# A two-layer hybrid decoder step on one core: adaLN slabs moved between stages, output projection in half contractions, attention scaling moved to another engine

## The chip, the core and the metric

The kernel runs on one core of one Trainium2 chip. The metric is the device time of one execution in microseconds (us); a measurement is the median over several executions. Engines: PE is TensorE (matrix products), DVE is VectorE, ACT is ScalarE, POOL is GpSimd, SP is SyncE, whose queue issues nearly all the weight loads. Each engine works through its own instructions in order.

## The reference

Two layers with the same structure, for 512 prompt tokens and 8 sample sequences of 4 tokens, model width 1024:

```python
mod = silu(c) @ w_ada + b_ada                     # adaLN: 1024 x 6144 per layer
sh1, sc1, g1, sh2, sc2, g2 = split(mod, 6)
h = rms_norm(x, norm1) * (1 + sc1) + sh1
q, k, v, u, xr, yg = split(h @ w_in)              # 1024 x 1536
o_attn = window_attention(q, k, v, sinks)         # 8 heads, window 128
o_ssm, o_lru = s5(u), rg_lru(xr, yg)
o = concat(rms_norm(o_attn), rms_norm(o_ssm), rms_norm(o_lru)) @ w_o
x = x + g1 * o
h2 = rms_norm(x, norm2) * (1 + sc2) + sh2
gate, val = split(causal_conv3(h2 @ w_up))        # 1024 x 5632
x = x + g2 * ((gelu(gate) * val) @ w_down)        # 2816 x 1024
```

## The kernel before

Activations lie with 128 features on the partitions, eight chunks of features, and 544 tokens (512 prompt, 32 sample) on the free axis, in two halves of 256 and 288 tokens. A float32 product is made from three products of rounded parts: weight `whi` with data `hh` and `hl`, weight `wlo` with data `hh` (`mm3`, line 430). One unit is 128 output features: 8 chunks x 3 products x 2 halves = 48 matmuls.

Weights come in the class `Weights`: SP loads 512 KB into one of three `raw` buffers (line 412), ACT casts it to `whi` (415), DVE subtracts to `wlo` (416), into one of six slots. When a unit is done its slot goes to the next weight in a fixed order.

The stages of a layer are: a preamble (layer 0 only: x, the first adaLN slabs, the norm); the mixer (12 units of the input projection with chains of attention, SSM and LRU work drawn in between, then the rest of these chains, here called the tail); the output projection (`proj`, 8 units x 2 halves; `KO` gives the order of its eight chunks of contraction: 6, 7, 4, 5 are SSM and LRU outputs, 0 to 3 attention outputs); and the ffn (44 units of the up-projection in three parts, and after each part a share of the down-projection).

The adaLN product is made of slabs: 512 KB of `w_ada` each, loaded into the same `raw` buffers, then four matmuls of 32 x 256 (line 524; a row of the trace counts one slab as x8). Eight slabs fill one result of 8 chunks, which ACT copies out (531), PE transposes (536) and DVE adds to the bias (543). There are 48 slabs per layer. Layer 0's first 16 are in the preamble, four of them loaded as pieces of 512 bytes (line 502). The remaining 32 of layer 0 and the first 16 of layer 1 are drawn between the work of mixer 0, the last 32 of layer 1 between the work of mixer 1 (`background`). The ffn has none.

In the attention, a unit is two heads by 128 queries. Its scores (matmul, line 1242) go through a masked maximum on DVE (1244), an exponential on ACT, a reciprocal on DVE (1251) and a scaling on DVE, which is two calls of `ts` (line 384), then to the transposes on PE (1263). One small copy for the sinks on DVE stands ahead of it (1241).

PSUM results that PE writes are named by bank: `mb0s`, `mb1s` (mixers), `fb0w`, `fb0s`, `fb1w` (ffn) and `wide`. The number in a name is the layer.

Of the kernel before, what the change touches and what calls it, by code (L numbers as in the profile page):

```python
# [19 lines left out]
L = 2  # L20
# [4 lines left out]
KC = 8  # L25
# [16 lines left out]
KO = (6, 7, 4, 5, 0, 1, 2, 3)  # L42
NATT = 1
AHEAD = 7
SPARE = (4, 5, 9, 11)
PIN = True
S12 = (2, 14, 5, 16)
SQN = (0, 10)
NHN = [9, 17]
S3 = 1  # L50
# [13 lines left out]

PRM = {}
_n = 0
for _name, _w in (
# [10 lines left out]
    "wada": (L, 3, 8, 2, 128, 4, 256), "win": (L, 12, 128, 8, 128), "wo": (L, 8, 128, 8, 128),  # L78
# [56 lines left out]
def layout(I):  # L135
# [43 lines left out]
    A["wada"] = I["w_ada"].reshape(L, 8, 128, 3, 4, 2, 256).transpose(0, 3, 1, 5, 2, 4, 6)  # L179
# [137 lines left out]
def trunk(ctx: ExitStack, tc: tile.TileContext, A, O):  # L317
# [173 lines left out]
    def ada_slabs(l, banks, ahead, spare=()):  # L491
        d = LY[l]
        todo = [(bank, k, hf) for bank in banks for hf in range(2) for k in range(8)]
        have = {}

        def fetch(n):
            if n < len(todo) and n not in have:
                bank, k, hf = todo[n]
                if n in spare:
                    have[n] = [T(512) for _ in range(2)]  # L500
                    for a, t in enumerate(have[n]):
                        nc.sync.dma_start(t.rearrange("p (g c) -> p g c", g=4),
                                          A["wada"][l, bank, k, hf, :, :, 128 * a:128 * a + 128])
                    return
                raw = wp.tile([128, 8, 128], F32, tag="raw", name="raw", bufs=NRAW)
                have[n] = raw.rearrange("p (g a) c -> p g (a c)", g=4)
                nc.sync.dma_start(have[n], A["wada"][l, bank, k, hf])

        for n, (bank, k, hf) in enumerate(todo):
            for m in range(n, n + ahead + 1):  # L510
                fetch(m)
            if k == 0:
                if bank == 0 and hf == 0:
                    d["mod"] = lp.tile([128, 48, 9], F32, name="mod")
                ps = one(256)
            if n in spare:
                for a, t in enumerate(have[n]):
                    for g in range(4):
                        T_.matmul(ps[32 * g:32 * g + 32, 128 * a:128 * a + 128], silu[:, k, :],
                                  t[:, 128 * g:128 * g + 128], start=False, stop=k == 7, skip_group_check=True)  # L520
                free(*have[n])
            else:
                for g in range(4):
                    T_.matmul(ps[32 * g:32 * g + 32], silu[:, k, :], have[n][:, g],  # L524
                              start=k == 0, stop=k == 7, skip_group_check=True)
            del have[n]
            yield 1
            if k < 7:
                continue
            row = W(256)  # L530
            S.copy(row, ps)
            PS.put(ps)
            yield 1
            pt = one(256)
            for c in range(2):
                T_.transpose(pt[:, c * 128:c * 128 + 128], row[:, c * 128:c * 128 + 128], eye)

            def part(t):
                return t[:, bank * 16:bank * 16 + 16].rearrange("p (g h c) r -> p g h c r", g=4, h=2)[:, :, hf]

            src = pt.rearrange("p (c g r) -> p g c r", c=2, g=4)[:, :, :, 0:9]
            b = d["prm"]("bada")[:, :, None].to_broadcast([128, 48, 9])
            V.tensor_tensor(part(d["mod"]), src, part(b), op=OP.add)
            PS.put(pt)
            d["ada"] = (bank, hf)
            for al, at, bk in (("al1", 8, 0), ("al2", 32, 2)):
                if bk == bank:
                    alpha(l, al, "norm" + al[2], at, hf)
            yield 1
# [300 lines left out]
    def norm_half(hf, al, sh):  # L850
# [3 lines left out]
        for c in KORD:  # L854
            t = W(w)
            V.tensor_mul(t, x[:, c, a:b], nr)
# [6 lines left out]
            V.tensor_sub(hs[c][1][:, a:b], t, f32(hs[c][0][:, a:b]))  # L863
            yield

    def norm_all(hf, al, sh):
        yield from norm_stats(hf)
        for _ in norm_half(hf, al, sh):
            pass
# [362 lines left out]
    def att_S(l, M, u):  # L1232
# [8 lines left out]
        V.tensor_copy(pm[:, :, nk:nk + 1], d["nsink"][:, c, :, None])  # L1241
# [10 lines left out]
        for g in range(2):  # L1252
            ts(pm[:, g, 0:nk], pm[:, g, 0:nk], st[:, 2, g:g + 1])
# [173 lines left out]
    bg = []  # L1427

    def background(n=1):
        for _ in range(n):  # L1430
            while bg:
                try:
                    next(bg[0])
                    break
                except StopIteration:
                    bg.pop(0)

    def flush():
        while bg:
            background()  # L1440

    def mixers(l, pool):
        d = LY[l]
        mod = d["mod"]
        sh1 = mod[:, 0:8]
        M = Mix()
        M.pool = pool
        M.win_done = M.back = False
        M.units, M.pipe, M.left = ([], []), [None, None], [8, 9]
        M.r, M.o, M.g, M.hl = {}, set(), [None, None], [None, None]  # L1450
# [4 lines left out]
        M.sq, M.part = {}, {}  # L1455
        M.kz = const("kz", (128, 2, NP), pool=pool)
        M.ks = const("ks", (128, NS), pool=pool)
        for g in range(2):
            G.memset(M.kz[64 - 64 * g:128 - 64 * g, g], 0.0)
# [352 lines left out]
```

## Time and profile before

| | |
|---|---|
| runs | 1328.3, 1330.35, 1334.8 us; median 1330.35 us |
| the profiled execution | 1335.0 us, span 1333.2 us |
| PE / DVE / ACT busy | 95% / 66% / 43% of the span |
| mean granted TensorE clock | 0.992 |
| preamble | 0 to about 65 us |
| mixer 0 and output projection | to about 296 us; tail from 191 to 244 us |
| ffn of layer 0 | about 296 to 698 us |
| mixer 1 and output projection | to about 930 us; tail from 843 to 878 us |
| ffn of layer 1 | to the end |

The profiled execution is the slowest of those shown, 0.35% above the median. Busy shares are means over stages; a stage is read from its own rows.

### The profile page before, as it was taken

The page shows a single profiled execution, that of the slowest core. Times are in us where ns is not written, and L with a number is a line of the kernel's source. Part 1 is how long each engine was busy: PE and PEld are TensorE (multiplying, and loading weights), DVE is VectorE, ACT ScalarE, POOL GpSimd, SP SyncE. Part 2 cuts the span into 40 slices and gives each one's busy share as a digit, 9 for nine tenths or more (in the row PEclk, how much of TensorE's full clock was granted, in tenths as well). Part 3 has the DMA queues.
Part 4 walks back from the last instruction along what each step waited for, and adds up shares of the span by engine and source line. Part 5 has one row for each costly group of instructions (what it writes and reads, how often), then busy time and mean ns, then how long its engine had stood idle before and what let it go on. Part 6 is the DMA issues. An engine that isn't in the chain of part 4 may idle for free.

```text
span 1333.2 us, 26368 instructions
## 1 busy us (share of the span) xinstructions
PE 1270.1 (95%) x10438; PEld 1164.8 (87%) x10438; DVE 881.8 (66%) x2583; ACT 576.5 (43%) x1112; POOL 48.8 (4%) x82
## 2 busy tenths in 40 slices
PE   4899988999999999999999999899999999999998
PEld 2666765799999999999998776679999999999998
DVE  8787885988774556456576877668865456545651
ACT  4557544356542343234354466545643234313430
POOL 0021010000020000000000001000000000000000
PEclk9899999999999999999999999999999999999999
DMA  8876677533343223334235846602322332233221
GB/s 294 279 265 215 191 252 229 178 111 118 93 135 125 85 86 87 97 93 115 76 108 180 268 142 203 191 14 90 110 81 86 96 95 74 86 97 94 85 72 51
DMA packets 72460, 178.24 MB, mean 134 GB/s; under 512 B 15584, under 2 KB 26752, under 8 KB 72336
## 3 DMA queue, kind: packets, MB, share of 16 engines
q1 hardware_dynamic: 65456, 162.08, 39.1%
q0 software_dynamic: 4960, 11.68, 2.5%
q10 hardware_dynamic: 1920, 2.79, 0.7%
q8 instruction: 82, 1.34, 0.4%
q14 instruction: 42, 0.34, 0.1%
HBM read 159.37 MB, written 14.34 MB: 130 GB/s over the span
## 4 chain that ended last, share of the span: by engine, by line
PE 83%; DMA 9%; DVE 5%; ACT 2%; issue 1%; POOL 0%; SPq 0%; DVEq 0%; POOLq 0%; ACTq 0%
PE wide L430 42%; PE fb1w L430 9%; PE fb0w L430 8%; DMA raw<-in_wada_dram 6%; PE fb0s L430 5%; PE fb1s L430 4%; PE mb0s L430 3%; PE mb1s L430 3%; PE mb0s L524 1%; PE mb1s L524 1%; DMA raw<-in_wo_dram 1%; DVE wlo L416 1%; DMA f<-in_ssmh_dram 1%; DMA tab_br<-f 1%; PE mb1s L1242 0%
## 5 line engine op out<-in xcount | busy, mean ns | idle before, releaser
L430 PE MATMUL wide<-hh,whi 128*128 128x288 f32 (+1 forms) x1360 | 400.3, 295 | 1.2 <-ACT hh L897 0.8
L430 PE MATMUL wide<-hl,whi 128*128 128x288 f32 (+1 forms) x1360 | 395.9, 291 | 0.0
L430 PE MATMUL wide<-hh,wlo 128*128 128x288 f32 (+1 forms) x1360 | 394.3, 290 | 0.0
L416 DVE TENSOR_TENSOR wlo<-raw,whi 128x1024 fp32r<-128x1024 f32 (+1 forms) x176 | 211.0, 1200 | 187.1 <-ACT whi L415 183.1
L415 ACT CAST whi<-raw 128x1024 fp32r<-128x1024 f32 (+1 forms) x176 | 180.4, 1029 | 274.8 <-PE wide L430 125.8
L430 PEld LDWEIGHTS wide<-hh,whi 128*128 128x128 f32 x1360 | 257.2, 189 | 18.3 <-issue 14.0
L430 PEld LDWEIGHTS wide<-hl,whi 128*128 128x128 f32 x1360 | 257.1, 189 | 6.3 <-issue 6.1
L430 PEld LDWEIGHTS wide<-hh,wlo 128*128 128x128 f32 x1360 | 259.2, 191 | 3.0 <-issue 3.0
L380 DVE SCALAR_TENSOR_TENSOR f<-wide,prm,f 128x511 f32<-128x511 f32 x236 | 100.2, 485 | 0.0
L430 PE MATMUL wide<-mid,whi 128*128 128x256 f32 (+1 forms) x526 | 99.8, 287 | 0.0
L430 PEld LDWEIGHTS wide<-mid,whi 128*128 128x128 f32 x526 | 82.4, 188 | 0.0
L897 ACT CAST mid<-f 128x544 fp32r<-128x544 f32 x44 | 28.5, 647 | 122.4 <-DVE f L1660 119.1
L430 PE MATMUL wide<-mid,wlo 128*128 128x256 f32 (+1 forms) x263 | 75.5, 287 | 0.0
L377 ACT ACTIVATE f<-f 128x544 f32<-128x544 f32 x50 | 33.0, 659 | 89.2 <-DVE f L1650 84.5
L430 PE MATMUL fb1w<-hh,whi 128*128 128x256 f32 (+1 forms) x240 | 69.4, 289 | 1.8 <-ACT hh L862 1.3
L430 PE MATMUL fb1w<-hl,whi 128*128 128x256 f32 (+1 forms) x240 | 69.4, 289 | 0.0
L430 PE MATMUL fb1w<-hh,wlo 128*128 128x256 f32 (+1 forms) x240 | 68.8, 287 | 0.0
L430 PE MATMUL fb0w<-hh,whi 128*128 128x256 f32 (+1 forms) x224 | 64.7, 289 | 1.6 <-ACT hh L862 1.1
L430 PE MATMUL fb0w<-hl,whi 128*128 128x256 f32 (+1 forms) x224 | 64.7, 289 | 0.0
L430 PE MATMUL fb0w<-hh,wlo 128*128 128x256 f32 (+1 forms) x224 | 64.3, 287 | 0.0
L430 PE MATMUL fb0s<-mid,whi 128*128 128x288 f32 (+1 forms) x326 | 62.9, 290 | 0.0
L430 PE MATMUL fb1s<-mid,whi 128*128 128x288 f32 (+1 forms) x308 | 59.1, 289 | 0.0
(612 smaller groups left out, 2542.2 us busy)
## 6 DMA issues: line engine op xcount, KB each, us to landing
raw<-in_wada_dram SPq DMA_DIRECT2D x92, 512.0 KB, 5.2
raw<-in_wup_dram SPq DMA_DIRECT2D x88, 512.0 KB, 3.5
raw<-in_wdn_dram SPq DMA_DIRECT2D x32, 448.0 KB, 3.3
raw<-in_win_dram SPq DMA_DIRECT2D x24, 512.0 KB, 4.2
raw<-in_wo_dram SPq DMA_DIRECT2D x16, 512.0 KB, 4.5
raw<-in_wdn_dram SPq DMA_DIRECT2D x16, 512.0 KB, 3.5
e<-q ACTq DMA_DIRECT2D x32, 68.0 KB, 4.6
out_ox_dram<-x SPq DMA_DIRECT2D x8, 272.0 KB, 2.1
```

What stands on the lines that cost most here:

```text
L377: return S.activation(out, in_, f, bias=bias, scale=scale, **kw)
L380: return V.scalar_tensor_tensor(out, a, s, b, op0=op0, op1=op1, **kw)
L415: S.copy(hi, raw)
L416: V.tensor_sub(lo, raw, f32(hi))
L430: T_.matmul(out, w[wi][:, k, :], r[ri][:, a:b], start=first and i == 0, stop=last and i == 2)
L524: T_.matmul(ps[32 * g:32 * g + 32], silu[:, k, :], have[n][:, g], start=k == 0, stop=k == 7, skip_group_check=True)
L897: S.copy(dst[0], src)
```

## The change

- **Slabs.** The layout of `w_ada` in memory becomes six parts of eight slabs per layer. Layer 0's parts 0 and 1 stay in the preamble, parts 2, 3 and 4 in mixer 0. Part 5 of layer 0 and all six parts of layer 1, 56 slabs, go to the up-projection of layer 0's ffn as 28 pairs: one load of 1 MB into one buffer `araw`, its eight matmuls at once, one step for each unit that ends. Mixer 1 has none.
- **First loads.** The 16 slabs of the preamble are loaded at once, into tiles that are free then (`q`, `kz`, `xc`, `gate`, `glu`, `e`, `f`), without pieces of 512 bytes; the second half of x follows the first eight. The rotation tables of the SSM (`ssm_rot(0)`) are issued on their engine after the first norm chunks, and the norm of the first half has a shorter form in `norm_all`.
- **Output projection.** Units 0 to 3 are accumulated in two parts: chunks 6, 7, 4, 5 first, which are added to x, and later chunks 0 to 3, added again. Their weights come as two loads of 256 KB. Units 4 to 7 are as before.
- **Attention.** The sinks' copy goes from DVE to ACT, and the scaling becomes an ACT activation (`Copy` with a per-partition scale).

```diff
+WO = ((4, 8, range(4)), (0, 4, range(4)), (0, 8, range(4, 8)))
...
+    def ada_pairs(l, parts, raw, bank):
...
+        def fetch(part, k):
+            nc.sync.dma_start(raw, A["wada"][l, part, k:k + 2].rearrange("k p g c -> p k g c"))
+
+        fetch(*todo[0])
+        yield 1
+        for n, (part, k) in enumerate(todo):
...
+            for i in range(2):
                 for g in range(4):
...
+                    T_.matmul(ps[32 * g:32 * g + 32], silu[:, k + i, :], raw[:, i, g],
+                              start=k + i == 0, stop=k + i == 7, skip_group_check=True)
+            if n + 1 < len(todo):
+                fetch(*todo[n + 1])
             yield 1
...
+            if k == 6:
+                yield from ada_end(l, part, ps)
...
-        V.tensor_copy(pm[:, :, nk:nk + 1], d["nsink"][:, c, :, None])
+        S.copy(pm[:, :, nk:nk + 1], d["nsink"][:, c, :, None])
...
-            ts(pm[:, g, 0:nk], pm[:, g, 0:nk], st[:, 2, g:g + 1])
+            act(pm[:, g, 0:nk], pm[:, g, 0:nk], AF.Copy, scale=st[:, 2, g:g + 1])
...
+            with tc.issue_after(LY[0]["first"]):
+                for _ in ssm_rot(0):
+                    pass
...
+        def some(i, hf, ks, last=True):
+            for k in ks:
+                need(k, hf)
+            o = one(HALF[hf][1] - HALF[hf][0], True, PLAST[0] if (i, hf) in PLAST[1] else ())
+            for k in ks:
+                part(o, i, hf, k, k == ks[0], k == ks[-1])
+            end(i, hf, o, last)
+            tick()
...
+        for i in range(4):
+            for hf in range(2):
+                if (i, hf) not in ((0, 0), (1, 0), (2, 0)):
+                    some(i, hf, KO[:4], False)
...
+                have = {k: ada_load(0, 0, k, homes[k]) for k in range(8)}
+                W_.ahead(GRP)
+                fetch_x(1)
...
-            bg.append(ada_slabs(l, (1, 2), 1))
+            if l == 0:
+                bg.append(ada_slabs(0, (2, 3, 4), 1))
...
+                if l == 0:
+                    bga.append(ada_pairs(0, (5,), raw, "fb0s"))
+                bga.append(ada_pairs(l + 1, range(6), raw, f"fb{l}s"))
```

SP's queue in the preamble, before and then of the change. In the names `x` is the input, `raw` and `f` hold slabs, and `in_win` is the input projection's weight.

```order
L1752 DMA x<-in_x_dram 128x4x256 x2
L1755 DMA eye<-in_eye_dram 128x128
L1756 DMA gm<-in_gm_dram 128x12
L507 DMA raw<-in_wada_dram 128x1024 x4
L502 DMA f_89<-in_wada_dram 128x4x128
L502 DMA f_90<-in_wada_dram 128x4x128
L502 DMA f_91<-in_wada_dram 128x4x128
L502 DMA f_92<-in_wada_dram 128x4x128
L507 DMA raw<-in_wada_dram 128x1024 x2
L412 DMA raw<-in_win_dram 128x1024 x3
L1752 DMA x<-in_x_dram 128x4x288 x2
```

```order
L1811 DMA x<-in_x_dram 128x4x256 x2
L1814 DMA eye<-in_eye_dram 128x128
L1815 DMA gm<-in_gm_dram 128x12
L530 DMA raw<-in_wada_dram 128x1024 x3
L526 DMA q<-in_wada_dram 128x512 x4
L526 DMA kz<-in_wada_dram 128x512 x2
L526 DMA xc_146<-in_wada_dram 128x512
L526 DMA xc_147<-in_wada_dram 128x512
L526 DMA gate<-in_wada_dram 128x512
L526 DMA glu<-in_wada_dram 128x512
L413 DMA raw<-in_win_dram 128x1024 x3
L1811 DMA x<-in_x_dram 128x4x288 x2
```

Ahead of the input projection's weights there were eight slabs, two of them in pieces, through four buffers; now there are eight through tiles of their own, and the other eight follow x.

SP's queue in layer 0's up-projection, of the change, with what each load waits for (a suffix of the semaphores' names is left as printed). `in_wup` is the up-projection's weight.

```order
L413 DMA raw<-in_wup_dram 128x1024 [waits DMAHW5_49,DVE_49,Activation_49]
L566 DMA araw<-in_wada_dram 128x2x1024 [waits PE_49]
L413 DMA raw<-in_wup_dram 128x1024 [waits DMAHW6_49,DVE_49]
L566 DMA araw<-in_wada_dram 128x2x1024 [waits DMAHW1_49,PE_49]
L413 DMA raw<-in_wup_dram 128x1024 [waits DMAHW7_49,DVE_49]
```

The loads of pairs wait for PE's matmuls on the pair before, and stand between loads of weights, which wait for DVE. Before the change this part of the queue has only the weights.

PE in the tail of mixer 1, before and then of the change. `kz`, `q` are an attention unit's scores, `eye,pm` the transposes of its probabilities, the rows of L430 and L431 the output projection.

```order
L430 MATMUL mb1s_7977<-hh_82,wlo_110 128x256
L524 MATMUL mb1s_7974<-raw,cin 32x256 x11
L1277 MATMUL wide_70<-g_7979,vt 64x128 x4
L1263 MATMUL mb1s_7975<-eye,pm 128x128 x2
L1242 MATMUL wide_71<-kz,q 128x512
L1359 MATMUL mb1s_7974<-f_93,f_90 32x128 x4
```

```order
L431 MATMUL mb1s_8112<-hh_82,wlo_114 128x288
L1317 MATMUL wide_70<-g_8114,vt 64x128 x4
L1303 MATMUL wide_71<-eye,pm 128x128 x2
L1282 MATMUL mb1s_8111<-kz,q 128x512
L431 MATMUL mb1s_8112<-hh_84,whi_115 128x288
L431 MATMUL mb1s_8112<-hl_85,whi_115 128x288
L431 MATMUL mb1s_8112<-hh_84,wlo_116 128x288
L431 MATMUL mb1s_8112<-hh_86,whi_115 128x288
```

Where slabs stood between the attention units, half contractions of the output projection stand now: five of 12 matmuls in each layer's tail, beside the three that were there.

## Rows read from the trace of the kernel before

**Rows 1.** The page, busy time and share of the span by engine

```profile
PE 1270.1 (95%) x10438; PEld 1164.8 (87%) x10438; DVE 881.8 (66%) x2583; ACT 576.5 (43%) x1112; POOL 48.8 (4%) x82
```

**Rows 2.** The page, chain that ended last, by engine

```profile
PE 83%; DMA 9%; DVE 5%; ACT 2%; issue 1%; POOL 0%; SPq 0%; DVEq 0%; POOLq 0%; ACTq 0%
```

**Rows 3.** Busy us (instructions) of each engine by stretch, clock, DMA

```profile
0.00:44.00 44.00, 21.89 (x180) 10.39 (x180) 35.65 (x209) 16.34 (x36) 3.58 (x10) 0.96 0.91 309
135.00:191.00 56.00, 52.99 (x490) 41.56 (x484) 47.49 (x181) 31.32 (x62) 3.64 (x4) 1.00 0.69 207
191.00:244.00 53.00, 43.98 (x425) 26.04 (x423) 33.77 (x150) 23.83 (x68) 2.10 (x2) 0.94 0.76 247
315.00:698.00 383.00, 382.68 (x3109) 381.85 (x3110) 231.65 (x501) 147.52 (x246) 12.52 (x23) 1.00 0.34 102
720.00:790.00 70.00, 64.47 (x624) 52.47 (x626) 51.87 (x140) 31.36 (x51) 4.75 (x8) 0.98 0.78 238
790.00:843.00 53.00, 51.56 (x416) 39.23 (x408) 38.44 (x143) 35.55 (x82) 4.71 (x4) 1.00 0.52 159
843.00:878.00 35.00, 28.54 (x238) 17.79 (x236) 25.12 (x107) 18.17 (x58) 0.00 (x0) 1.00 0.49 155
```

**Rows 4.** The same for line 430 alone, in the two tails

```profile
191.00:244.00 53.00, 4.94 (x25) 4.03 (x23) 0.94 0.76 247
843.00:878.00 35.00, 4.85 (x36) 4.46 (x36) 1.00 0.49 155
```

**Rows 5.** The same for line 524 alone (slab matmuls)

```profile
48.00:191.00 143.00, 19.85 (x200) 5.05 (x200) 0.99 0.73 229
191.00:244.00 53.00, 14.64 (x160) 4.26 (x160) 0.94 0.76 247
700.00:843.00 143.00, 18.63 (x192) 4.58 (x192) 0.99 0.63 195
843.00:878.00 35.00, 5.71 (x64) 1.82 (x64) 1.00 0.49 155
```

**Rows 6.** TensorE's waits, 48 to 300 us, then 700 to 935

```profile
PE mb0s L524 <- DMA raw<-in_wada_dram: 7.3, 6, 2.4
PE mb0s L1263 <- DVE pm L384: 3.8, 3, 1.5
PE wide L524 <- DMA raw<-in_wada_dram: 1.3, 1, 1.3
...
PE mb1s L524 <- DMA raw<-in_wada_dram: 9.3, 10, 1.7
```

**Rows 7.** Timeline: one slab, and two in a row

```profile
72.07 0.64 PE L524 MATMUL mb0s<-raw,cin 128*32 128x256 f32 x8
...
219.44 1.07 PE L524 MATMUL wide<-raw,cin 128*32 128x256 f32 x16
```

**Rows 8.** Chain of waits in the up-projection, start, us, what

```profile
451.00 6.01 PE fb0w L430 x48
```

**Rows 9.** Lines, 48:300, then two of 135:300 by shape

```profile
L377 ACT ACTIVATE half<-half,mod,al 128x256 f32<-128x256 f32 x16 | 8.9, 595 | 1.3 <-DVE half L856 1.1 <-DVE al L380 0.2
L384 DVE TENSOR_SCALAR pm<-pm,st 128x256 f32<-128x256 f32 (+1 forms) x32 | 9.4, 332 | 0.1
...
L1265 ACT COPY f<-wide 128x256 f32<-128x256 f32 x1 | 0.4, 372 | 0.1
L380 DVE SCALAR_TENSOR_TENSOR x<-mb0s,mod,x 128x256 f32<-128x256 f32 x12 | 5.7, 482 | 3.9 <-PE mb0s L430 3.7
```

**Rows 10.** The page, DMA issues: count, KB each, us to landing

```profile
raw<-in_wada_dram SPq DMA_DIRECT2D x92, 512.0 KB, 5.2
raw<-in_wup_dram SPq DMA_DIRECT2D x88, 512.0 KB, 3.5
raw<-in_wdn_dram SPq DMA_DIRECT2D x32, 448.0 KB, 3.3
```

**Rows 11.** TensorE's waits, 0 to 66 us

```profile
PE wide L524 <- DMA raw<-in_wada_dram: 10.7, 4, 8.9
```

More of the change, by code (lines that the diff above doesn't have):

```diff
@@ L496, in fetch, with ada_slabs @@
+    def ada_slabs(l, parts, ahead, have=None):
+        d = LY[l]
+        todo = [(part, k) for part in parts for k in range(8)]
+        have = have or {}
         def fetch(n):
             if n < len(todo) and n not in have:
[L498 to L509, printed above, removed]
+                have[n] = ada_load(l, *todo[n])
+        for n, (part, k) in enumerate(todo):
             for m in range(n, n + ahead + 1):
@@ L512, in ada_slabs @@
             if k == 0:
-                if bank == 0 and hf == 0:
+                if part == 0:
                     d["mod"] = lp.tile([128, 48, 9], F32, name="mod")
                 ps = one(256)
[L516 to L522, printed above, removed]
+            for g in range(4):
+                T_.matmul(ps[32 * g:32 * g + 32], silu[:, k, :], have[n][g // 2][:, g % 2],
+                          start=k == 0, stop=k == 7, skip_group_check=True)
@@ L530, in ada_slabs @@
[L530 to L549, printed above, removed]
+            if k == 6:
+                yield from ada_end(l, part, ps)
     def alpha(l, al, n, at, hf):
@@ L1466, in mixers @@
             setattr(M, n, const(n, sh, pool=pool))
+        return M
+    def mixers(l, M):
+        d = LY[l]
+        mod = d["mod"]
+        sh1 = mod[:, 0:8]
+        M.win_done = M.back = False
+        M.units, M.pipe, M.left = ([], []), [None, None], [8, 9]
+        M.r, M.o, M.g, M.hl = {}, set(), [None, None], [None, None]
+        M.sq, M.part = {}, {}
+        for g in range(2):
+            G.memset(M.kz[64 - 64 * g:128 - 64 * g, g], 0.0)
+        AR.names.update((t.tensor.name, t) for t in M.xt)
         CH = M.CH = Chains()
@@ L1549, in need, with part, end @@
             raise RuntimeError(("never ready", k, hf, M.left))
-        def end(i, hf, o):
+        def part(o, i, hf, k, first, last):
+            a = 0 if i > 3 or k < 4 else 4
+            mm3(o, W_[("wo", l, a, i)], k - a, hs[k], HALF[hf], first, last)
+        def end(i, hf, o, last=True):
             with urgent():
@@ L1566, in proj @@
         for i, hf in skewed(GRP):
[L1567 to L1574 removed]
+            some(i, hf, KO if i > 3 else KO[4:])
             if (i, hf) == (7 - SKEW, 1):
```

169 lines of the change are left out of this document (101 added, 68 removed).

## The prediction, made before the change was run

> **What bounds the kernel now.** I read the page first. TensorE is busy 95% of the span [rows 1], and the chain of waits puts 83% on it, 9% on transfers, 5% on DVE [rows 2]. So the time falls by PE work or PE waits removed, and rises by PE work added, unless the stage has room. The windows by stage show where there is room [rows 3]: none in the up- and down-projection of layer 0 (382.68 of 383 us); 3 of 56 us in the first part of mixer 0; 9 of 53 us in its tail; 5.5 of 70 us and 1.4 of 53 us in mixer 1, and 6.5 of 35 us in its tail. In the preamble PE is busy half the time and the transfers 0.91. In both tails the output projection's matmuls take only 4.9 us [rows 4]: what runs there is chains and slabs. The waits name the cause of much of the idle time, transfers of slabs that come late: 7.3 + 1.3 us in mixer 0, 9.3 us in mixer 1 [rows 6].
>
> **Slabs out of the mixers.** PE's cost of one slab is the matmul time of line 524 over its slabs, at x8 each [rows 5]: 14.64/20 = 0.73 us in mixer 0's tail, 18.63/24 = 0.78 before mixer 1's tail, 5.71/8 = 0.71 in it. I use 0.77 where I count slabs.
> Mixer 0 keeps 24 of 48 slabs, and the 24 removed are its last ones: 20 in the tail, the rest just behind it. That is 14.6 + 4 x 0.77 = 17.7 us of work and up to 8.6 us of waits [rows 6].
> Mixer 1 loses all 32: 24 ahead of the tail with 18.63 us and 9.3 - 3.7 = 5.6 us of waits, 8 in the tail with 5.71 us and the 3.7 us of waits that fall there [rows 6].
>
> **Half contractions into the tails.** Five of 12 matmuls each move from behind a tail into it. One unit of 48 takes 6.01 us [rows 8], so these are 5 x 12 x 6.01/48 = 7.5 us per layer. They shorten what follows by 7.5 us; the tail lengthens only where PE has no room.
> Mixer 0's tail, limited by PE alone: 43.98 - 14.64 + 7.5 = 36.8 us in place of 53. With what is saved behind it (7.5 + 3.1) the bound is 16.2 + 10.6 = 26.8 us. DVE, however, is busy 33.77 us of this tail and ACT 23.83 [rows 3], and the attention units are serial chains: I let PE wait 7 us of the new tail, and take **-20**. Bounds: the tail keeps its 53 us (-10.6), or is limited by PE alone (-26.8).
> Mixer 1's tail in the same way: 28.54 - 5.71 + 7.5 = 30.3 of 35 us, and 7.5 behind it: -12.2. Ahead of the tail up to 18.63 + 5.6 = 24.2 us could go. DVE's 51.87 + 38.44 us in these 123 us would then fill 90 of 99, so I keep 18 of the 24: **-30**. Bounds: half of the 24.2 and a tail of 35 us (12.1 + 7.5 = -19.6), or all (-36.4).
>
> **Pairs into the up-projection.** Two slabs in a row take 1.07 us against 0.64 for one [rows 7]; with 0.13 us of change to and from the other matmuls (0.77 - 0.64), a pair is 1.2 us. 28 pairs: 33.6 us. The seven ends have two transposes each; at 6.01/48 = 0.125 us for a matmul [rows 8] and with some change again, 7 x 0.3 = 2 us. PE is full here [rows 3], so nothing hides it: **+36**. The copies, DVE additions and the 28 MB of load have room (DVE 232, ACT 148 of 383 us, transfers 0.34).
> There is one new wait. `araw` is a single buffer, so the next 1 MB is issued only when PE has read the last, and PE comes back after one unit, 6.01 us. No row has a load of 1 MB. From 448 to 512 KB the landing grows from 3.3 to 3.5 us [rows 10], so 512 KB more adds 1.6: 5.1 us, and 5.4 with 0.3 to issue. Two weight loads one after the other would be 7.0; two slab loads 10.4, a figure of the busy mixers, whose transfers are at 0.7. I take 5.1, as the up-projection's transfers are at 0.34, and the wait at nothing; the margin is 0.6 us. Behind the waiting load in SP's queue stand the weights of a later unit, which are fetched six slots ahead, about five units or 30 us: hidden.
> The Trainium skill (DMA: Bandwidth & Descriptors, section "Bandwidth") has 1 MB at 6.15 us; by it, with the issue, each pair that follows a pair would be about 0.4 us late, and the sum 9 us higher. Its figure is for loads issued from GpSimd, and no run shown here has such a load.
>
> **Scaling on ACT.** Per layer 32 scalings (332 ns mean, 9.4 us counted in mixer 0) and 16 small copies leave DVE [rows 9]. ACT has no such row. Below, a copy of 128 x 256 takes 372 ns; above, an activation with two per-partition operands 595 ns [rows 9]. It has one such operand, so I take 0.45: 14 us more on ACT per layer, which has over half its time free in mixers, and about 11 us less on DVE, the busier one. The chain of one unit gets 2 x (0.45 - 0.33) = 0.24 us longer. PE waited for these scalings 3.8 us in mixer 0 [rows 6]; if nothing covers it, the eight of 16 units that I put in a tail cost 2 us per layer, 4 us in all; below, DVE's queue ahead of the scaling vanishes, about -2. In the sum +1, with the next piece.
> The Trainium skill speaks against this move (ScalarE: Activation LUTs, section "Rules for kernel authors"): multiplications belong on VectorE. The rows agree on the duration, since nothing in ACT's rows of this shape is as short as 332 ns; by the rule the change would lose the 4 us above, by the rows on free time nearly nothing.
>
> **Extra residuals.** Eight more per layer on DVE (482 ns for 256 tokens [rows 9]): 4 us per layer, beside PE's matmuls, and DVE has lost 11 us. If uncovered, the sum rises by 4 us in each layer; taken with the above at **+1**.
>
> **Preamble.** The bytes stay; pieces of 512 bytes go; the loads start without waiting for buffers. PE waited 10.7 us for slabs there, 8.9 of them for the first [rows 11], and the transfers are at 0.91 [rows 3], so little can be had: **-4**. Bounds: -8 (the other waits and a shorter norm chain), and +2 where the second half of x, now ahead of eight slabs, makes them late.
>
> **Sum** against the profiled 1335.0 us: -4 - 20 - 30 + 36 + 1 = -17, so 1318. That execution is 0.35% above the median of 1330.35, and in the same ratio the change stands at **1313 us** as a median.
>
> **Rivals.**
> *The pairs come late.* The loads land at 7.0 us, not 5.1. After each fourth pair two steps have none; the other 21 pairs follow another at once and each then waits 1.0 to 1.3 us: +21 to +27, and 1334 to 1340 us: slower at its upper end. It decides from a landing of about 6.8 us on (0.8 us late, 17 us in all). For it: slabs have landed at 5.2 us instead of 3.5 for the same bytes. Against: that is where transfers are at 0.7. By the figure of the Trainium skill named above this rival would give 1322 us.
> *The chains hold the mixers.* DVE and the serial attention chain keep the tails as long as they are, and half the gain ahead of mixer 1's tail is lost: -10.6 - 19.6 - 4 + 36 + 1 = +3, 1333 us, no change. For it: DVE 47.49 of 56 us and 33.77 of 53. Against: DVE itself loses 11 us per layer. A piece of it is the clock, 0.94 in mixer 0's tail [rows 3], where PE had waited: with less to do it may be lower.
> *All the room is used.* -8 - 26.8 - 36.4 + 36 - 2 = -37, 1293 us. For it: no engine but PE is full in any row.
>
> **How the numbers follow.** A measurement of this kernel tells about 0.5%, 6.6 us, from no change. Chances: the forecast 0.62, all the room 0.05, late pairs 0.15, chains 0.18. The forecast and the best case are faster; of the late pairs 0.10 is slower and 0.05 the same; of the chains 0.13 is the same, 0.04 slower, 0.01 faster. That is 0.68 faster, 0.18 the same, 0.14 slower. The likeliest alone ranges from 1302 to 1323. The range reaches from 1299, near the best case, to 1336, which takes in the chains and half of the late pairs.
>
> **What would show it.** Right: 35 to 37 us longer from the first `fb0w` to the first `mb1s`, with PE still full and no wait for `araw`; mixer 1 from there to the first `fb1w` shorter by 25 to 33 us; mixer 0 shorter by 15 to 25. Wrong: waits for `araw` of over 10 us in the sum; tails as long as before with PE idle and waiting for `pm` or ACT; a preamble that ends later than before.

## The result, and the profile after

The change is slower: 1341.5 us (median of 11 runs, 1337.8 to 1344.4) against 1330.87 us (11 runs). The ratio is 1.0073, 95% interval 1.0054 to 1.0092. The forecast was 1313, range 1299 to 1336.

From the page of the change: busy time, chain that ended last, and the landing of the new loads.

```profile
PE 1275.7 (95%) x10406; PEld 1173.5 (88%) x10406; DVE 871.8 (65%) x2521; ACT 599.7 (45%) x1196; POOL 48.7 (4%) x82
...
PE 63%; DVE 4%; ACT 3%; DMA 2%; issue 1%; POOL 0%; SPq 0%; DVEq 0%; POOLq 0%; ACTq 0%
...
araw<-in_wada_dram SPq DMA_DIRECT2D x28, 1024.0 KB, 5.2
```

TensorE's share is unchanged [rows 1], but 5.6 us more of it is busy, and a pair's 1 MB lands in 5.2 us, where I had estimated 5.1. The windows by stage (columns as in rows 3):

```profile
0.00:44.00 44.00, 26.33 (x180) 14.11 (x180) 36.04 (x217) 20.18 (x46) 1.25 (x6) 0.88 0.82 299
190.00:232.00 42.00, 35.57 (x278) 26.45 (x279) 28.99 (x130) 26.21 (x72) 0.00 (x0) 0.84 0.09 24
232.00:280.00 48.00, 48.00 (x387) 47.82 (x386) 47.37 (x146) 22.35 (x40) 1.67 (x3) 1.00 0.45 149
280.00:299.00 19.00, 15.31 (x112) 13.99 (x112) 14.58 (x51) 10.07 (x23) 0.54 (x1) 0.91 0.41 125
299.00:714.00 415.00, 410.17 (x3510) 389.36 (x3509) 229.17 (x497) 143.89 (x237) 11.46 (x21) 1.00 0.48 158
724.00:790.00 66.00, 62.31 (x538) 58.34 (x537) 57.55 (x173) 38.61 (x71) 2.22 (x4) 1.00 0.47 140
790.00:837.00 47.00, 44.57 (x388) 36.98 (x387) 34.18 (x121) 34.96 (x88) 7.24 (x8) 1.00 0.34 87
837.00:877.00 40.00, 32.12 (x211) 22.98 (x210) 26.91 (x94) 28.96 (x85) 0.00 (x0) 0.91 0.20 57
877.00:939.00 62.00, 59.22 (x422) 53.62 (x420) 47.94 (x150) 32.97 (x77) 0.00 (x0) 0.92 0.21 61
```

The up-projection is full as before. The tail of mixer 0, here 190 to 232, is about 11 us shorter than in [rows 3], that of mixer 1, 837 to 877, is 5 us longer. The granted clock is 0.84 in the tail of mixer 0, 0.91 in that of mixer 1, 0.91 at the start of the ffn (280 to 299) and 0.92 from 877 to 939; the tails had 0.94 and 1.00 [rows 3]. And DVE is busy 47.37 of 48 us in mixer 0's output projection. TensorE's waits over the whole span:

```profile
PE mb0s L551 <- DMA raw<-in_wada_dram: 6.6, 6, 2.7
PE wide L479 <- DVE qr L381: 3.8, 3, 2.0
PE fb0s L577 <- DMA araw<-in_wada_dram: 3.4, 3, 1.6
...
PE fb0w L431 <- ACT hh L903: 2.4, 1, 2.4
```

Three numbers by stage, from the first `fb0w`, `mb1s` and `fb1w` matmuls: to the first `fb0w` 279.8 us (before 295.7), from there to `mb1s` 444.2 (403.8), from there to `fb1w` 214.9 (230.4). So -15.9, +40.4 and -15.6, and the rest -1.3. Of the signs of being right, mixer 0 shows its 15 to 25 us, barely and with the preamble in it; the second stage is over its 35 to 37 us and mixer 1 far below its 25 to 33. Of the signs of being wrong, mixer 1 shows one: its tail is not shorter.

One number of the prediction, the 3.7 us of slab waits in the tail of mixer 1 before, has no row in [rows 6]; it is this one, from TensorE's waits of the kernel before, 843 to 878 us:

```profile
PE mb1s L524 <- DMA raw<-in_wada_dram: 3.7, 4, 1.2
```

For what follows I also number the matmuls of the weight products (line 430, and 431 or 434 later), 48 to a unit, 172 units, and compare when each kernel starts a given unit. Units 0 to 11 are the input projection of layer 0, 12 to 19 its output projection, 20 on its ffn, 86 on mixer 1, 98 to 105 its output projection. Differences to the kernel before in us, one profiled execution each:

```
unit          change  f1   g1    f2    f3    f4    g2
  4            -4.0  -0.2  -0.3  -4.0  -0.9  -6.2  -0.9
 11            -4.5  -1.3  -2.6  -4.4  -2.1  +1.5  -1.6
 13           -16.9  -9.9 -14.9 -16.0  -1.4  +6.7  -3.4
 20           -19.6 -12.4 -17.4 -18.6  -1.0  +6.6  -3.4
 22           -14.4 -12.3 -17.3 -12.5  -0.1  +6.7  -3.4
 86           +23.3 +24.0 +20.0 +24.0  -0.1  +6.7 +16.3
 97            -3.3  -3.6  -7.0  -3.1  +0.4  +4.2 -10.9
101            +0.9  -0.2  +2.5   0.0  +1.4  +4.7  -5.6
103            +7.8  -0.2  +2.6  +5.7  +7.7  +4.7  -5.6
112            +8.1  -0.4  +2.4  +5.5  +7.8  +4.5  -5.8
```

f1: pairs alone. g1: pairs and scaling on ACT. f2: pairs, scaling and halves. f3: scaling and halves alone. f4: new loads and delayed rotation tables alone. g2: pairs for mixer 1 alone. All are described below.

### The profile page after: what moved, and what is told of

Its sections match the earlier page's. It is cut to its first block, busy times and chain, and to the rows that moved or that the text cites. A ratio compares the mean times of both kernels' runs of the same rounds, so it can differ in the third digit from the quotient of the medians.

```text
span 1340.8 us, 26252 instructions
## 1 busy us (share of the span) xinstructions
PE 1275.7 (95%) x10406; PEld 1173.5 (88%) x10406; DVE 871.8 (65%) x2521; ACT 599.7 (45%) x1196; POOL 48.7 (4%) x82
## 3 DMA queue, kind: packets, MB, share of 16 engines
q1 hardware_dynamic: 64096, 162.08, 37.7%
## 4 chain that ended last, share of the span: by engine, by line
PE 63%; DVE 4%; ACT 3%; DMA 2%; issue 1%; POOL 0%; SPq 0%; DVEq 0%; POOLq 0%; ACTq 0%
PE wide L431 33%; PE fb1w L431 9%; PE fb0w L431 7%; PE fb1s L431 4%; PE mb1s L431 3%; PE fb0s L431 3%; PE fb0s L577 2%; DMA araw<-in_wada_dram 1%; ACT pm L378 1%; PE mb1s L1282 1%; DVE f L381 1%; DMA f<-kscr 0%; ACT whi L416 0%; ACT L378 0%; PE mb1s L1121 0%
## 5 line engine op out<-in xcount | busy, mean ns | idle before, releaser
L431 PE MATMUL wide<-hh,whi 128*128 128x256 f32 (+1 forms) x1368 | 402.0, 295 | 5.0 <-ACT hh L937 2.0
L431 PE MATMUL wide<-hl,whi 128*128 128x256 f32 (+1 forms) x1368 | 399.6, 292 | 0.0
L431 PE MATMUL wide<-hh,wlo 128*128 128x256 f32 (+1 forms) x1368 | 396.9, 290 | 0.0
L417 DVE TENSOR_TENSOR wlo<-raw,whi 128x1024 fp32r<-128x1024 f32 (+2 forms) x184 | 212.1, 1153 | 195.8 <-ACT whi L416 191.9
L416 ACT CAST whi<-raw 128x1024 fp32r<-128x1024 f32 (+2 forms) x184 | 182.4, 991 | 317.6 <-PE wide L431 171.9
L431 PEld LDWEIGHTS wide<-hh,whi 128*128 128x128 f32 x1368 | 258.9, 190 | 21.1 <-issue 11.2
L431 PEld LDWEIGHTS wide<-hh,wlo 128*128 128x128 f32 x1368 | 261.2, 191 | 2.5 <-issue 2.3
L431 PEld LDWEIGHTS wide<-hl,whi 128*128 128x128 f32 x1368 | 259.7, 190 | 4.0 <-issue 3.6
L431 PE MATMUL wide<-mid,whi 128*128 128x256 f32 (+1 forms) x582 | 111.3, 288 | 0.0
L431 PEld LDWEIGHTS wide<-mid,whi 128*128 128x128 f32 x582 | 91.4, 188 | 0.4 <-issue 0.4
L431 PE MATMUL wide<-mid,wlo 128*128 128x256 f32 (+1 forms) x291 | 83.8, 288 | 0.0
L431 PE MATMUL fb1w<-hh,whi 128*128 128x256 f32 (+1 forms) x240 | 69.3, 289 | 2.0 <-ACT hh L903 1.5
L431 PE MATMUL fb1w<-hl,whi 128*128 128x256 f32 (+1 forms) x240 | 69.5, 290 | 0.0
L431 PE MATMUL fb1w<-hh,wlo 128*128 128x256 f32 (+1 forms) x240 | 68.9, 287 | 0.0
L431 PE MATMUL fb0w<-hh,whi 128*128 128x256 f32 (+1 forms) x224 | 66.0, 295 | 2.4 <-ACT hh L903 2.4
L381 DVE SCALAR_TENSOR_TENSOR x<-wide,mod,x 128x256 f32<-128x256 f32 x53 | 25.6, 483 | 63.4 <-PE wide L431 63.3
L431 PE MATMUL fb0w<-hl,whi 128*128 128x256 f32 (+1 forms) x224 | 65.0, 290 | 0.0
L431 PE MATMUL fb0w<-hh,wlo 128*128 128x256 f32 (+1 forms) x224 | 64.7, 289 | 0.0
L378 ACT ACTIVATE pm<-pm,st 128x256 f32<-128x256 f32 (+3 forms) x128 | 57.4, 476 | 11.3 <-DVE st L1284 9.2
```

Of the source, the lines that this page charges most:

```text
L378: return S.activation(out, in_, f, bias=bias, scale=scale, **kw)
L381: return V.scalar_tensor_tensor(out, a, s, b, op0=op0, op1=op1, **kw)
L416: S.copy(hi, raw)
L417: V.tensor_sub(lo, raw, f32(hi))
L431: T_.matmul(out, w[wi][:, k, :], r[ri][:, a:b], start=first and i == 0, stop=last and i == 2)
```

## The experiments

Ratios are to the kernel before on the same chip, with 95% intervals. Theories when I began: **A**, slabs had filled gaps in the mixers, so removing them frees little; **B**, scaling on ACT lengthens the attention chain; **C**, the halves cost more than they fill. **D** (lost clock in the mixers) and **E** (the new preamble) came up after the first runs.

**One part undone at a time.** e1: scaling and sinks' copy back on DVE.

```diff
-        S.copy(pm[:, :, nk:nk + 1], d["nsink"][:, c, :, None])
+        V.tensor_copy(pm[:, :, nk:nk + 1], d["nsink"][:, c, :, None])
...
-            act(pm[:, g, 0:nk], pm[:, g, 0:nk], AF.Copy, scale=st[:, 2, g:g + 1])
+            ts(pm[:, g, 0:nk], pm[:, g, 0:nk], st[:, 2, g:g + 1])
```

> The change with the scaling of the probabilities and the sinks' copy back on DVE. If the mixers' length is set by chains whatever engine scales (theory A: slabs had been filling TensorE's gaps there, and the chains hold the stages), within 4 us of the change, 1338 to 1345. If the scaling on ACT has made the attention units' chain longer (theory B), 8 us or more come back: 1333 or less, with the tail of mixer 1 shorter by 5 us.

1.0067 (1.0041 to 1.0093): as the change. B seemed to be out; g1 shows where it holds.

e2: the output projection whole.

```diff
-WO = ((4, 8, range(4)), (0, 4, range(4)), (0, 8, range(4, 8)))
+WO = ((0, 8, range(8)),)
...
+        for k in KO:
+            need(k, 0)
+            for i in range(GRP):
+                part(o[i], i, 0, k, k == KO[0], k == KO[-1])
```

> The change with the output projection of all units in one accumulation. Theory A and my prediction: the half contractions fill the tails, so without them up to 7.5 us per layer come behind the tails: 1345 to 1356. Theory C (the halves cost more than they fill, by extra loads, residuals and waits at the stage's end): 1335 or less.

1.0093 (1.007 to 1.0116): neither the 7.5 us per layer nor a loss. In this and in every kernel with the projection whole nothing is lost from unit 101 to 103, and in every one with halves 5.7 to 7.0 us are.

e3: slabs back in the mixers; e4: slabs left out.

```diff
-                bga.append(ada_pairs(l + 1, range(6), raw, f"fb{l}s"))
...
+            bg.append(ada_slabs(l, (2, 3, 4, 5), 1))
...
+                bg.append(ada_slabs(l + 1, (0, 1), 1))
```

> The change with the 56 slabs of the pairs back in the mixers, one by one (24 in mixer 0, 32 in mixer 1), and none in the up-projection. The up-projection gets about 40 us shorter by the trace of the change. Theory A (in the mixers the slabs took mostly gaps, so that their place there costs about 25 to 30 us): 1326 to 1332. By my prediction's prices of slabs in the mixers (27 + 34 us with waits): 1355 or more.

```diff
-                bga.append(ada_pairs(l + 1, range(6), raw, f"fb{l}s"))
+                V.memset(LY[0]["mod"][:, 40:48], 0.1)
...
+                V.memset(e["mod"], 0.1)
```

> The change without the 56 slabs of the pairs at all: their modulation is a constant, and the up-projection has no load, matmul or end of a pair. The price of the pairs where they are: by my prediction 36 us (1305), by the cumulative count of the matmuls in the trace of the change about 38 to 40 us (1301 to 1304). The difference of this run to the one with the slabs in the mixers is what the same slabs cost there: 25 to 30 us by theory A, 55 to 60 us by my prediction.

1353.2 us, 1.0155 (1.0127 to 1.0184), and 1311.7 us, 0.9853 (0.983 to 0.9875). The 56 slabs cost 41.5 us in the mixers and 29.8 us as pairs, so the pairs are the better place within this change. The 41.5 us are neither the 25 to 30 of A, which falls in the form I gave it, nor the 55 to 60 of my prices.

**Several parts undone.** e5: pairs, new preamble and short norm alone; e6: new preamble and short norm alone; e8: the same without slabs. Their edits are those above, put together.

> The change with the scaling on DVE and the output projection whole, both undone together: what stays is the pairs and the preamble. Alone, undoing the scaling moved the time by -0.6 us and undoing the halves by +1.2. If they do not touch each other, 1342 us. If the chains hold the tails unless both DVE is relieved and TensorE has other work there, both together are worth more: 1347 or more.

> The kernel before with the preamble of the change alone: scaling on DVE, projection whole, the 56 slabs in the mixers one by one. The run with halves, scaling on ACT and slabs in the mixers took 1353, 22 us more than before. If halves and scaling do harm where slabs still fill TensorE's gaps, this is 1326 (before, less the 5 us that the preamble gains up to the fourth unit). If the preamble and the order of its loads do the harm, 1345 or more.

> As the run without pairs, with scaling on DVE and the projection whole: no slab of the 56 anywhere (the modulation is a constant). Its difference to the run with loads only is the price of the slabs in the mixers without halves, its difference to the run with pairs and loads their price in the up-projection (36 us if nothing else moves). If the mixers' gaps take slabs for nearly nothing there, the first difference is under 30 us and this run over 1296; by my prediction's prices it is 54 to 60 us, and this run 1270.

1.0109 (1.0086 to 1.0132), 1.0125 (1.0091 to 1.0159), 0.9831 (0.9798 to 0.9864). e5 lies between its two cases, e6 is its second, and e8 is neither. The surprise is e6: preamble and short norm alone cost 17 us on the kernel before. Slabs in the mixers cost 1347.6 - 1306.9 = 40.7 us without halves too, pairs 38.3.

**Cover for the attention's norm.** e7, one constant.

```diff
-SKEW = 4
+SKEW = 5
```

> The change with one constant: the second halves of the output projection start one unit later (skew 5 for 4; it holds for the last share of layer 0's down-projection too), so that 24 more matmuls of first halves, 2.8 us, stand before the first matmul that needs the attention's norm of the second half. If the halves' loss of 6 to 7 us at the end of mixer 1's projection is cover taken from that norm: 3 to 7 us faster than the change, 1335 to 1339, and no wait for the norm's reciprocal root there. If the loss is DVE's extra residuals: no difference.

1.0138 (1.0107 to 1.0168): slower than the change, and the loss at units 101 to 103 stayed (6.9 us). But the 24 matmuls did not come to stand where I meant them: in mixer 1 of both traces 24 weight matmuls lie between the attention's last product with v and the transposes of its norm, and TensorE's two waits there, 1.59 and 1.04 us, are the same. So this run says nothing on whether cover is missing.

**Work that no output needs.** e9: 56 slabs' matmuls on rows that are resident, whose results nothing reads:

```diff
+    def fill(n, rows):
+        for i in range(n):
...
+            for g in range(4):
+                T_.matmul(ps[32 * g:32 * g + 32], silu[:, i % 8, :], rows[:, 0:256],
+                          start=i % 8 == 0, stop=i % 8 == 7, skip_group_check=True)
...
+            bg.append(fill((24, 32)[l], M.cos))
```

> The change with work added that no output needs: 24 slabs' matmuls in mixer 0 and 32 in mixer 1, on rows that lie in SBUF already, without any load, drawn in where the slabs were before. If TensorE bounds the mixers, they cost what slabs cost there, 0.73 us each: 41 us, 1382. If they fall into gaps and keep the clock up (theory D: the change is slow because its mixers run for 38 us at half clock after 60 us, before 10), under 20 us, at most 1360, with a mean clock of 0.99.

1.0108 (1.0063 to 1.0154), clock 0.987 in the profiled run and 0.989 as the mean of its five. Their rows in mixer 1, by line:

```profile
L565 PE MATMUL mb1s<-cos,cin 128*32 128x256 f32 x256 | 20.8, 386 | 0.0
```

That is 0.65 us for each slab, 36 us for 56, and the time rose by 0.35%, 4.7 us, give or take 0.5%. So TensorE's part of a slab costs at most about a third of its length in these mixers. That most of the 41 us that slabs cost there comes with their loads and ends is argued from this; no run shows it. This is the part of A that holds.

**The preamble.** e10: old loads with the rotation tables at once; e11: only the tables at once; e12: only the long norm.

```diff
-                ad = ada_slabs(0, (0, 1), 0, have)
+                ad = ada_slabs(0, (0, 1), AHEAD, SPARE)
...
-            with tc.issue_after(LY[0]["first"]):
-                for _ in ssm_rot(0):
-                    pass
+            for _ in ssm_rot(0):
+                pass
...
-        for _ in norm_half(hf, al, sh, True):
+        for _ in norm_half(hf, al, sh):
```

> The change with the preamble of before: slabs loaded seven ahead through the three buffers and four pairs of free tiles, x's second half and the first weights where they were, the rotation tables issued at once. The run with only the new preamble was 17 us slower than before. If the preamble is the cause (theory E), about 15 us come back: 1324 to 1330, below the kernel before. If the loss is in the mixers whatever the preamble (theory D): 1345, the change and the 4 us that the preamble gained.

> The change with the rotation tables of the SSM issued at once, the one wait that its preamble adds. If their delay holds the SSM chains of mixer 0 back (a part of theory E), 5 us or more faster: 1336 or less. If not, within 3 us of 1341.

> The change with the norm of the first half in its longer form everywhere. The short form makes the first half ready earlier, and TensorE then waits longer for the second half (2.4 us at the start of either mixer's follower, and half clock after it). If that is worth something: 3 to 6 us faster, 1335 to 1338. If not: 1341 to 1343.

1.0067 (1.0043 to 1.0091), 1.0104 (1.0068 to 1.014), 1.0041 (1.0014 to 1.0068). E falls for the whole change. The long norm is worth some 4 us, at the edge of what the intervals tell apart.

**The missing corners.** The next four combine the edits above on the code of before.

> The kernel before with the pairs alone: 56 slabs as pairs in the up-projection, everything else as before. If new loads and short norm cost 17 us wherever they are, as in the run with them alone: 1345 - 17 = 1328. If they only hurt where the slabs are in the mixers: 1341 to 1345, so that pairs alone cost 10 us or more on the kernel before, because its mixers gave slabs place for less than 36 us.

> The change with both the preamble and the norm of before: pairs, halves and scaling on ACT stay. From the two runs that took one of them back (old preamble 1.0067, old norm 1.0041, the change 1.0073): 1.0035, 1335 to 1337. If the two together matter more than their sum: 1328 or less.

> The kernel before with halves and scaling on ACT alone, slabs in the mixers as before. By my prediction the halves shorten each layer by up to 7.5 us where TensorE has room: 1316 to 1322. If slabs and halves compete for the same gaps: 1331 to 1338, no gain or a loss.

> The kernel before with the new loads and the delayed rotation tables alone, the norm in its longer form. If the short norm made the 17 us: 1328 to 1332. If the loads and the delay did, by starting the mixer 5 us earlier against slab loads that come no earlier: 1343 to 1347.

f1 0.9992 (0.9976 to 1.0007), f2 1.0096 (1.0072 to 1.012), f3 1.0084 (1.005 to 1.0117), f4 1.004 (1.0014 to 1.0066). Pairs alone change nothing; halves and scaling lose with the pairs and without them. f2 and f3 are slower than either of their cases, and f4 lies between its two.

**Which of the two, and a better share of pairs.** g1 is f1 with the scaling on ACT. g2 keeps mixer 0's slabs there:

```diff
-                    bga.append(ada_pairs(0, (5,), raw, "fb0s"))
-                bga.append(ada_pairs(l + 1, range(6), raw, f"fb{l}s"))
+                bga.append(ada_pairs(l + 1, range(2, 6), raw, f"fb{l}s"))
```

> Pairs alone (0.9992) with the scaling and the sinks' copy on ACT, output projection whole, preamble and norm as before. If the halves are what costs 0.84 to 1.04% in the runs with both (by keeping TensorE from the last attention units, and by the residuals that fill DVE): 0.997 to 1.000, 1326 to 1331. If the scaling on ACT does: 1.007 or more.

> Pairs alone, but only the 32 slabs of mixer 1 as 16 pairs in the up-projection; the 24 of mixer 0 stay there one by one. By the stages of the run with pairs alone: mixer 1 -24 us as there, up-projection 16/28 of 36.4 = +20.8, mixer 0 as before: -3.4 us, 0.9975, below both kernels if it holds. If the slabs' price in a mixer depends on how the mixer before it ended, and the stages do not add: 1.000 or more.

g1 1.0035 (1.0013 to 1.0056), g2 0.9941 (0.9919 to 0.9962). g1 lies between its two cases. g2, 1324.3 us, is faster than both kernels, by more than twice the 3.4 us that I had expected.

## Why the prediction was wrong, step by step

The ratios make two chains from the kernel before to the change, each step the difference of two ratios above, with an interval of 0.3 to 0.4% to either side where both are measured:

```
before -> f1 -> g1 -> f2 -> change   pairs -0.08%, scaling +0.43%, halves +0.61%, preamble and norm -0.23%
before -> e6 -> e5 -> e1 -> change   preamble and norm +1.25%, pairs -0.16%, halves -0.42%, scaling +0.06%
```

So the pairs are worth nothing clear on either. Halves with scaling, and preamble with norm, cost about 1% each when they come first, and nothing or a little less than nothing when they come second. I had forecast -14 us (-1.05%) for the first group and -4 us for the second. Neither order gives that: the best case measured is -0.36% for the first (e5 to the change), 4.8 us, give or take 4.

**Pairs into the up-projection, +36: right.** f1 goes from -12.4 at unit 20 to +24.0 at unit 86, 36.4 us. (The 40.4 us of the change, counted from the first `fb0w`, hold 4 us more, most of them lost by the halves at units 21 and 22.) Leaving the pairs out gave 29.8 and 38.3 us over the whole kernel. The chain of waits of the change, around 650 us, shows two pairs around one unit:

```profile
644.66 1.00 PE fb0s L577 x16
645.66 6.21 PE wide L431 x48
651.86 1.00 PE fb0s L577 x16
```

1.00 + 6.21 us against the 6.01 of [rows 8]: 1.2 us a pair. The rival that they come late did not come true: TensorE waited 3.4 us in three places. The Trainium skill (DMA: Bandwidth & Descriptors, section "Bandwidth") has 6.15 us for 1 MB, for loads issued from GpSimd; these, issued from SP, landed in 5.2 us (median), and for them the trace decides.

**Slabs out of the mixers: right in size, not in place.** Without the 7.5 us of halves in each, my -20 and -30 are -12.5 and -22.5. f1 shows -12.4 at unit 20, and -24.2 from unit 86 to 103. But in mixer 1 all of it comes ahead of the tail (-27.6 by unit 97), and the tail, which I had made 4.7 us shorter, got 3.4 us longer from unit 97 to 103, without its slabs. TensorE is not what holds it, being busy 30.96 of 38 us (window below). That the size came out is luck in mixer 1, where two errors cancel, and in mixer 0, where a trace is known only to some 9 us (see the preamble). Pairs alone bring nothing: 36 for 36, as my own terms had it. The gain that I forecast stood on the other parts, above all on the halves.

**Half contractions, -15 (7.5 us per layer): the step that failed.** "They shorten what follows by 7.5 us; the tail lengthens only where PE has no room" came true in neither layer. Three pairs of kernels differ in the halves alone: g1 and f2, e5 and e1, e2 and the change. They give +8.1, -5.6 and -2.7 us, each give or take 4 to 5, so -15 is out in all three; C, that they cost more than they fill, is clear on the first alone. By stage of the traces, to unit 22 and from 86 to 103, they give +4.8 and -1.0, +1.2 and -2.5, -3.3 and +0.3, for my -7.5 and -7.5. (The trace of f2 is its fastest execution, 5 us below its median; that much of the +8.1 stands in no trace.)

In mixer 1 the matmuls did move. TensorE's timeline in g1, without halves: the last scores, the last product with v, the transposes of the norm's reciprocal root, and what follows these:

```profile
889.66 1.02 PE L1285 MATMUL wide<-kz,q 128*128 128x512 f32 x2
...
895.54 0.66 PE L1320 MATMUL mb1s<-f,vt 128*64 128x128 f32 x8
...
900.60 0.43 PE L482 MATMUL wide<-eye,qr 128*128 128x128 f32 x2
900.78 0.38 PE L434 MATMUL wide<-hl,whi 128*128 128x288 f32 x1
```

and in f2, with halves (the last row is the first matmul that needs this norm):

```profile
889.93 1.02 PE L1285 MATMUL mb1s<-kz,q 128*128 128x512 f32 x2
...
899.24 0.66 PE L1320 MATMUL mb1s<-f,vt 128*64 128x128 f32 x8
...
905.04 0.43 PE L482 MATMUL wide<-eye,qr 128*128 128x128 f32 x2 [1.59 <-DVE qr L384]
906.51 0.57 PE L434 MATMUL mb1s<-hh,whi 128*128 128x288 f32 x1 [1.04 <-ACT hh L940]
```

Mixer 1 begins 4.0 us later in f2 (unit 86). Counted from there, the last product with v comes after 177.6 us in g1 and 177.2 in f2 (174.2 and 172.0 in e5 and e1, 179.1 and 178.8 in e2 and the change): the halves do not delay this last link of the attention, and bring it forward by 0.3 to 2.2 us. By then they have done 42 more of the numbered matmuls, which is 5.3 us of TensorE at 6.01/48. Yet from this product to unit 104 all twenty kernels take 21.7 to 23.0 us, with halves or without. The windows between these two points, in g1 and then in f2:

```profile
895.50:917.70 22.20, 22.09 (x177) 21.56 (x177) 17.04 (x52) 7.76 (x15) 0.00 (x0) 1.00 0.23 72
```

```profile
899.20:920.80 21.60, 18.78 (x136) 17.40 (x136) 17.73 (x54) 8.19 (x17) 0.00 (x0) 0.92 0.19 58
```

TensorE is full in g1. In f2 it has 41 matmuls less, is idle 2.8 us, 1.6 + 1.0 of them in the two waits above, and its granted clock behind them is lower, 0.92 in the mean for 1.00, which is another 1.7 us. In g1 the work that stands in that place, second halves that do not need the attention's norm, covers it; with halves this work has gone ahead. So the step had the path wrong: behind the last link the attention's norm sets the time as soon as TensorE has less to do, and the matmuls moved ahead free nothing. No run gave f2 that cover back.

In layer 0 the matmuls did not get into the tail. The weight products from 192 us to the last product with v, in g1 and then in f2:

```profile
192.00:226.20 34.20, 5.14 (x24) 4.25 (x24) 0.90 0.19 50
```

```profile
192.00:226.30 34.30, 4.37 (x24) 3.44 (x24) 0.85 0.10 23
```

There are 24 in both. The next weight product in f2, ahead of all half contractions, has to wait for its data:

```profile
228.67 0.39 PE L434 MATMUL wide<-hh,whi 128*128 128x256 f32 x1 [1.99 <-ACT hh L940]
```

So the half contractions come behind the last product with v, where TensorE is full (48.00 of 48 us in the change), and what is said above of each layer's tail holds for mixer 1 alone. And at units 20 to 22 layer 0 loses 6.1 us: -18.6 to -12.5 in f2, where g1 has -17.4 and -17.3. Window of the output projection of layer 0 in g1:

```profile
233.00:278.40 45.40, 45.40 (x363) 45.22 (x362) 41.44 (x133) 21.14 (x43) 2.21 (x4) 1.00 0.26 82
```

the same in f2:

```profile
234.00:281.00 47.00, 46.79 (x373) 46.26 (x372) 46.19 (x141) 24.45 (x45) 1.67 (x3) 1.00 0.50 163
```

f2's wait behind it, from TensorE's waits of 280 to 300 us:

```profile
PE fb0w L434 <- ACT hh L906: 2.4, 1, 2.4
```

and the windows of 281 to 300 us, in g1 and then in f2:

```profile
281.00:300.00 19.00, 18.89 (x161) 17.04 (x160) 16.10 (x55) 13.27 (x26) 0.00 (x0) 1.00 0.53 166
```

```profile
281.00:300.00 19.00, 16.06 (x112) 14.89 (x112) 13.02 (x52) 9.72 (x23) 0.54 (x1) 0.82 0.29 97
```

DVE goes from 41.44 of 45.4 us to 46.19 of 47; then TensorE waits for the second half of the norm, and its clock is 0.82 for 1.00. I had put the eight more residuals at nothing, as hidden beside TensorE. That a full DVE delays the last residual and the second half's norm is argued from these rows. No run took the residuals alone away, and they are not all that is new there: from 230 to 281 us f2 has 2.4 us more of residuals than g1, and 3.7 us more of weight subtractions (`wlo`).

**Scaling on ACT, +1: a term that is two.** It cost 5.7 us, give or take 4, on f1 (g1), and nothing clear in the two other pairs that differ in it alone (e1 to the change +0.06%, e5 to e2 -0.16%). By stage all three agree: to unit 22 they gain 5.0, 9.3 and 4.8 us, and from 86 to 103 they lose 6.9, 7.7 and 4.9. So B is right for mixer 1 and wrong for mixer 0. The duration was estimated at 0.45 us and measured 0.496:

```profile
L378 ACT ACTIVATE pm<-pm,st 128x256 f32<-128x256 f32 x12 | 5.4, 496 | 0.3 <-DVE st L1291 0.3
```

What I missed is the chain that ends mixer 1. The same three rows in f1, to be held against those of g1 above:

```profile
886.92 1.02 PE L1285 MATMUL wide<-kz,q 128*128 128x512 f32 x2
...
892.67 0.66 PE L1320 MATMUL mb1s<-f,vt 128*64 128x128 f32 x8
...
897.73 0.43 PE L482 MATMUL wide<-eye,qr 128*128 128x128 f32 x2
```

Counted from unit 86, the last product with v comes after 170.7 us in f1 and 177.6 in g1, 6.9 us later; in e1 and the change after 172.0 and 178.8, in e5 and e2 after 174.2 and 179.1. So it is the scaling on ACT, not the halves, that delays the last link. The chain of waits by line, 825 to 900 us, in f1 and then in g1:

```profile
by line: PE wide L434 18.8%; PE mb1s L434 14.5%; PE mb1s L1285 10.7%; PE mb1s L1320 6.9%; DVE pm L1287 4.6%; PE wide L1285 4.1%; PE mb1s L1306 3.5%; DVE hl L941 2.5%; PE mb1s L1437 2.5%; PE wide L1306 2.5%; DVE xc L384 2.3%; ACT pm L381 2.1
```

```profile
by line: PE mb1s L434 15.5%; ACT pm L381 12.6%; PE mb1s L1285 10.9%; PE wide L434 10.4%; PE mb1s L1320 7.0%; DVE pm L1287 3.5%; ACT L381 3.4%; PE wide L1285 2.6%; PE mb1s L1437 2.4%; ACT half L381 2.1%; ACT f L1308 2.0%; issue 2.0%; ACT g L
```

A window in the tail of mixer 1, again f1 and then g1:

```profile
842.00:880.00 38.00, 30.96 (x205) 20.53 (x206) 30.92 (x125) 22.10 (x73) 0.00 (x0) 0.96 0.12 32
```

```profile
842.00:880.00 38.00, 32.63 (x182) 21.17 (x181) 23.38 (x91) 24.21 (x81) 0.00 (x0) 0.82 0.10 30
```

ACT's work on `pm`, exponential and scaling together, rises from 2.1% to 12.6% of the chain, 1.6 to 9.4 of 75 us, and the granted clock of this window falls from 0.96 to 0.82, worth 5.3 us of full clock. How much of the 6.9 us is chain and how much is clock, no run separates. The share of free time on ACT, by which I called the move covered, says nothing of a chain that goes through ACT twice for each head. The Trainium skill's rule (ScalarE: Activation LUTs, section "Rules for kernel authors") that multiplications belong on VectorE held in the one and not in the other.

**Preamble, -4.** The new loads do gain 4 to 6 us up to the fourth unit (change, f4), and lose them before the tail of mixer 0 ends (f4: +6.7 at unit 13). Alone they cost 0.4%, with the short norm 1.25%, and in the whole change nothing. That the parts do not add is shown by the two chains; why, is open. One thing bears on it: the scheduler's order of mixer 0 is another in each of these kernels. e5 and e8, with the same code up to the ffn, already differ in TensorE's 544th matmul, at some 94 us, and reach unit 20 at -6.9 and -15.5 us. So a stage of one trace is known to some 9 us in mixer 0, and which part "is" the 1% there cannot be said from these runs.

**The clock (D), a piece of a rival.** The mean granted clock was 0.982 over the runs of the change, and 0.991 over the runs of before that stand beside e1 to e4 (0.988 to 0.989 beside the later ones). It does not follow the slabs alone: f1, without them in the mixers, has 0.983, and e3, with them, 0.981. D is not the cause of the loss by itself: f1 takes as long as the kernel before, and e9 has the clock back at 0.989 and is no faster for it.

**The sum by stage.** To unit 22 the trace of the change has -14.4 us, to 86 +37.7, to 103 -15.5; my terms were -24 (preamble and mixer 0), +36 and -30, with +1 for scaling and residuals. Together that is +8 for -17, 25 us off. The halves are 19 of these 25 by g1 and f2, and 12 to 14 by the two other pairs.

**The rivals.** "The chains hold the mixers" is the nearest: it named the tails, the attention chain and the clock, and gave 1333 us, but as gains withheld, with the 7.5 us of the halves still in both layers. Its -14.6 for preamble and mixer 0 against -14.4 is luck: it lets the slabs save 3.1 us there and the halves 7.5, where f1 shows 12.3 for the slabs alone and no pair 7.5 for the halves. That scaling would lengthen the attention chain by more than 2 us per layer, or that halves would free nothing, was in no case of mine, and the range ended 5.5 us short. What decided was priced near nothing, or as a full gain, under one argument, that the free time of an engine settles it: the halves by TensorE's free time in the tails, the residuals by DVE's, the scaling by ACT's.

## What to carry to other kernels

In a stage whose end is a serial chain, ask of each moved operation which link of the chain it lengthens; a share of free time over the stage does not hide it. Before counting a gain for work moved forward into a tail, look whether its inputs are ready there, and what sets the time behind the last link once that work is gone: it may have been the cover of the next wait. Compare kernels that differ in one part only, and count from the start of the stage: beside f1, the halves seemed to delay the attention by 6.5 us, which g1 shows to be the scaling. Price a move at both ends by stage, and move only where the stages differ: here 32 of 56 slabs were worth moving (0.9941), all of them were not (0.9992).

## What the runs showed of the hardware

Added matmuls of 36 us in all cost 4.7 us, give or take 0.5% of the time, in mixers where TensorE was busy 80 to 95% by the windows of the change. A short wait cost more than its length: in f2, behind waits of 1.6 and 1.0 us, the window from 899.2 to 920.8 us has a granted clock of 0.92, where g1, which does not wait there, has 1.00. And the tail of mixer 1 ran at a granted clock of 0.96 in f1 and of 0.82 in g1: 182 matmuls took 32.63 us of TensorE in g1, more than the 30.96 us of 205 in f1, while its idle time was shorter, 5.4 against 7.0 us. What lowered the clock there, these rows do not show.
